# An encoder layer on one core: dummy products ahead of the first sums, and another order of loads and products for the second pair of row tiles

## The chip, the core and the metric

The kernel runs on one core of a Trainium2 chip. The metric is the device time in microseconds (us) of one execution, median over runs. Engines are named as in the profile: PE (TensorE, matrix products), ACT (ScalarE), DVE (VectorE), POOL (GpSimd), and SP, whose queue issues most DMA transfers.

## What is computed

One encoder layer on x of 1024 rows by 2048 columns, all in 32-bit floats. What matters here is its beginning:

```python
mod = jax.nn.silu(c) @ w_ada + b_ada
shift, scale, gate = jnp.split(mod, 3, axis=-1)
h = rmsnorm(x, pre_g) * (1.0 + scale[:, None]) + shift[:, None]
proj = h @ w_in
```

Then come windowed attention, pooling, a gated merge and a product with w_out; the change touches none of them.

## The kernel before, in words

Products keep single precision by splitting each operand into a high part, rounded to the format that PE takes at full speed (fp32r), and a low part, the rest; a product is high by high, high by low and low by high. Most of proj is made with Strassen's seven products of blocks (line 237). Ahead of that stands a ramp, in which data arrive while PE is already at work: for the first weight tiles of 256 columns (called tile i here, i = 0 to 3), plain blocks (line 833) are made from the first four row tiles of the weights, k = 0 to 3, taken as pair one (k = 0, 1; j = 0 in the code) and pair two (k = 2, 3; j = 1). The 1024 rows of x form two halves, s = 0 and 1, of 512. A block is named by weight half and x half: "11", "21" (x half 0), "12", "22" (x half 1); one block of one tile and one pair is six products of 512 columns.

Before the operands can be made, the scale is needed by columns of w_ada: `row_sums` multiplies silu(c) with w_ada on PE (tiles GEMV, line 539, four column groups), ACT copies the sums (acc, line 543), PE turns them (PM, line 523), DVE adds them up (pm, line 525) and makes `modc` (line 550). This is done for pair one and, by `scales[1]`, for pair two.

x is turned by PE (`turn_part`, tile XT, line 502, 128x128 transposes into a PSUM bank) and taken out by `take_turned` to the SBUF tiles xT (ACT line 510, DVE line 508). `raw_operands` multiplies by the scale column: the high part on ACT (B11h, B21h, B12h, B22h; line 695), the low part on DVE (B11l and so on; line 696). With `turned=True` it reads the PSUM bank, else the copy xT. `wide_weights` splits weights: high part whi on ACT (line 816) or DVE (814), low part wlo on DVE (line 106). `square_of` sums squares of x for the norm, on ACT (line 457) or DVE (454). `hold` copies a finished block from PSUM (line 837). The line `root` (931) makes ACT load its square-root table early.

`keep` pins an instruction: pinned instructions of an engine stand in the order of the calls. Each engine works through its own queue in order, and SP issues loads in the order of the calls, eight in flight. Loads are called in this order: 8 tiles of w_ada for the first scale, x columns 0 to 255 of rows 0 to 511 in four loads, half of the first weights, whole quarters (512 columns) of x of rows 512 to 1023, columns 256 to 511 of rows 0 to 511, the other half of the weights, 8 tiles for the second scale, the weights of pair two (`fetch_wide(0, 1)`), further x.

## Time and profile before

| | |
|---|---|
| time, median of 3 runs | 2085.4 us (2083.93 to 2087.7) |
| the profiled execution: time | 2086.17 us |
| its span, first to last instruction | 2084.4 us |
| PE busy | 2067.4 us, 99% |
| DVE, ACT busy | 1567.6 us (75%), 1110.7 us (53%) |
| mean granted clock of TensorE | 0.999 |

The span leaves out what lies around the instructions. Busy shares are of the span. The ramp's part that the change rewrites is the first 35 us or so.

### The profile page before, as it was taken

How to read it: one execution, taken by the hardware profiler on the slowest of the kernel's cores; microseconds unless marked ns; L12 is line 12 of the kernel's file. 1: busy time of each engine (PE TensorE's matmuls, PEld its weight loads, DVE VectorE, ACT ScalarE, POOL GpSimd, SP SyncE). 2: the span in 40 equal slices, each digit the busy share in tenths (PEclk: the TensorE clock that was granted, in tenths of full speed). 3: DMA queues.
4: the chain of work that ended last, by engine and by line, in shares of the span. 5: the costliest groups of instructions: out<-in, count | busy, mean ns of one | idle time of the engine just before them, and what ended most of it. 6: DMA issues, size and time to landing. Idle time of an engine off the chain costs nothing.

```text
span 2084.4 us, 29055 instructions
## 1 busy us (share of the span) xinstructions
PE 2067.4 (99%) x9527; PEld 1701.9 (82%) x9527; DVE 1567.6 (75%) x2823; ACT 1110.7 (53%) x2120; POOL 37.7 (2%) x132
## 2 busy tenths in 40 slices
PE   8999999999999999999999999999999999999998
PEld 6778888888888888888888888888888888888886
DVE  5889778776565876777777688857868977889667
ACT  5764444444664634655665444334645644768554
POOL 0100000000000000000000000010000000000000
PEclk9999999999999999999999999999999999999999
DMA  9978877887665477655554577665655556786897
GB/s 341 358 268 265 276 245 246 296 288 228 201 217 176 152 263 255 200 164 178 184 168 147 183 228 227 209 235 194 228 173 162 180 193 202 228 305 207 294 334 248
DMA packets 303137, 476.61 MB, mean 229 GB/s; under 512 B 24026, under 2 KB 140402, under 8 KB 302984
## 3 DMA queue, kind: packets, MB, share of 16 engines
q1 hardware_dynamic: 297616, 459.89, 67.3%
q0 software_dynamic: 4304, 12.75, 1.6%
q10 hardware_dynamic: 1064, 2.11, 0.3%
q8 instruction: 75, 1.23, 0.2%
q14 instruction: 78, 0.64, 0.1%
HBM read 346.70 MB, written 130.05 MB: 229 GB/s over the span
## 4 chain that ended last, share of the span: by engine, by line
PE 93%; DMA 3%; DVE 2%; ACT 1%; issue 0%; SPq 0%; DVEq 0%; ACTq 0%
PE Z L237 31%; PE V L237 20%; PE X L237 20%; PE Z L1704 2%; PE Z L1706 2%; PE Z L1705 2%; PE X L1706 1%; PE X L1704 1%; PE X L1705 1%; PE V L1704 1%; PE V L1705 1%; PE V L1706 1%; PE PB L833 1%; PE PT L1414 1%; DMA xt<-in_x_dram 1%; PE PV L1425 0%
## 5 line engine op out<-in xcount | busy, mean ns | idle before, releaser
L96 ACT ACTIVATE whi<-raw 128x512 fp32r<-128x512 f32 (+1 forms) x528 | 314.9, 600 | 488.6 <-PE Z L237 253.0
L97 DVE TENSOR_TENSOR wlo<-raw,whi 128x512 fp32r<-128x512 f32 (+1 forms) x528 | 339.9, 649 | 140.2 <-PE Z L237 109.9
L97 DVE TENSOR_TENSOR wlo<-wr,whi 128x512 fp32r<-128x512 f32 x224 | 150.5, 689 | 51.2 <-ACT whi L96 48.1
L96 ACT ACTIVATE whi<-wr 128x512 fp32r<-128x512 f32 x224 | 138.4, 629 | 87.3 <-DVE wlo L97 30.0
L103 DVE TENSOR_TENSOR raw<-raw,raw 128x512 f32<-128x512 f32 x76 | 52.4, 690 | 81.3 <-DMA raw<-in_w_merge_dram 51.6
L96 ACT ACTIVATE whi<-ws 128x512 fp32r<-128x512 f32 (+1 forms) x88 | 53.0, 602 | 72.9 <-PE X L237 61.4
L237 PE MATMUL Z<-T1h,whi 128*128 128x512 f32 x328 | 89.7, 390 | 0.3 <-ACT u L251 0.3
L237 PE MATMUL Z<-B22h,whi 128*128 128x512 f32 x328 | 89.6, 392 | 0.0
L237 PE MATMUL Z<-T2h,wlo 128*128 128x512 f32 x328 | 88.9, 390 | 0.6 <-DVE wlo L97 0.6
L237 PE MATMUL X<-B21h,whi 128*128 128x512 f32 x328 | 89.5, 391 | 0.0
L237 PE MATMUL V<-T4h,whi 128*128 128x512 f32 x328 | 89.5, 392 | 0.0
L237 PE MATMUL X<-B11h,whi 128*128 128x512 f32 x328 | 89.4, 390 | 0.0
L237 PE MATMUL Z<-T2h,whi 128*128 128x512 f32 x328 | 89.0, 390 | 0.4 <-ACT Z L293 0.3
L237 PE MATMUL V<-T3h,whi 128*128 128x512 f32 x328 | 89.3, 391 | 0.0
L237 PE MATMUL X<-B11l,whi 128*128 128x512 f32 x328 | 89.2, 390 | 0.0
L237 PE MATMUL Z<-B22l,whi 128*128 128x512 f32 x328 | 88.9, 390 | 0.0
L237 PE MATMUL Z<-T1l,whi 128*128 128x512 f32 x328 | 88.9, 389 | 0.0
L237 PE MATMUL X<-B21l,whi 128*128 128x512 f32 x328 | 88.9, 390 | 0.0
L237 PE MATMUL V<-T3l,whi 128*128 128x512 f32 x328 | 88.9, 390 | 0.0
L237 PE MATMUL V<-T4l,whi 128*128 128x512 f32 x328 | 88.9, 390 | 0.0
L237 PE MATMUL V<-T4h,wlo 128*128 128x512 f32 x328 | 88.8, 390 | 0.0
L237 PE MATMUL X<-B11h,wlo 128*128 128x512 f32 x328 | 88.8, 390 | 0.0
(421 smaller groups left out, 4910.3 us busy)
## 6 DMA issues: line engine op xcount, KB each, us to landing
part<-part_d SPq DMA_DIRECT2D x136, 256.0 KB, 4.7
ada<-in_w_ada_dram SPq DMA_DIRECT2D x128, 256.0 KB, 5.6
raw<-in_w_merge_dram SPq DMA_DIRECT2D x64, 512.0 KB, 5.2
wr<-ws_dS SPq DMA_DIRECT2D x60, 512.0 KB, 5.4
raw<-in_w_in_dram SPq DMA_DIRECT2D x56, 512.0 KB, 4.3
wr<-in_w_out_dram SPq DMA_DIRECT2D x48, 512.0 KB, 5.2
proj_d<-part SPq DMA_DIRECT2D x68, 256.0 KB, 2.4
sw<-in_w_out_dram SPq DMA_DIRECT2D x64, 256.0 KB, 5.2
```

The source lines that it names most:

```text
L96: ins = (nc.scalar.activation(hi, src, AF.Copy), nc.vector.tensor_tensor(lo, src, f32(hi), ALU.subtract))
L97: nc.vector.tensor_tensor(lo, src, f32(hi), ALU.subtract))
L103: return (eng or nc.vector).tensor_tensor(o, a, b, ALU.add)
L237: nc.tensor.matmul(ps, w_[:, i], op[mov][j][m_], start=fresh and i == 0 and n == 0, stop=i == nj - 1 and n == 2, skip_group_check=True)
L833: keep(nc.tensor.matmul(opened[i, blk], w[:, kh, nt * P:(nt + 1) * P], mov[kh][m], start=j == n == 0, stop=j == 1 and n == 5, skip_group_c ...
L1414: nc.tensor.transpose(pt[:, i * P:(i + 1) * P], p[:, i * P:(i + 1) * P], ident)
L1704: nc.tensor.matmul(pb, hi, w[0], start=first, stop=False, skip_group_check=True)
L1705: nc.tensor.matmul(pb, lo, w[0], start=False, stop=False, skip_group_check=True)
L1706: nc.tensor.matmul(pb, hi, w[1], start=False, stop=last, skip_group_check=True)
```

## The change

- `ones` is filled by DVE ahead of `scz`, not by POOL. `warm` (products of the tile `ones` with itself, 128x128, results unused) moves up and is called with 6 ahead of the turning of c, 3 behind it, and 1 after each of the first two steps of the first sums.
- The first sums are turned ahead of the x transposes, and `sum_columns` turns them into the free part of the sums' own PSUM bank.
- All x quarters 0 are loaded in halves of 256 columns. The second halves move behind the second scale: rows 0 to 511 ahead of the weights of pair two, rows 512 to 1023 behind them.
- The first weights are split by row tile (`first_weights`), and the products of pair one are reordered around the transposes of x half 1.
- Tile 1's blocks of pair one ("11", and "21" in two parts) stand ahead of and behind the second sums. Pair two's transposes move behind the second sums, its operands are read from the PSUM banks (`turned=True`), its weights are split by DVE, and its blocks "11", "21" of tile 0 stand among the transposes. The squares of x quarter 0 follow.

The core of the diff:

```diff
+    ones = xa2.tile([P, P], F32, name="ones")
+    nc.vector.memset(ones, 1.0)
     nc.vector.memset(scz, 0.0)
-    ones = xa2.tile([P, P], F32, name="ones")
-    nc.gpsimd.memset(ones, 1.0)
...
+    warm(6)
     pc = bank(SEEDED[1], "pc")
...
+    warm(3)
     scales = [fetch_scales(0)]
-    fetch_halves(0)
+    fetch_halves(range(4), 0)
     fetch_wide(0, 0, 0, 256)
-    for si in range(4, 8):
-        fetch_row(si, (0,))
-    fetch_halves(1)
+    fetch_halves(range(4, 8), 0)
     fetch_wide(0, 0, 256, 512)
...
     scales.append(fetch_scales(1))
+    fetch_halves(range(4), 1)
     fetch_wide(0, 1)
+    fetch_halves(range(4, 8), 1)
...
+    def first_weights(kh):
+        if kh == 0:
+            weights0[0, 0] = [wp.tile([P, 2, 256], F32R, tag=t, name=uid(t), bufs=4) for t in ("whi", "wlo")]
+        hi, lo = (t[:, kh] for t in weights0[0, 0])
+        keep(nc.vector.tensor_copy(hi, wide[0, 0][:, kh, 0:256]))
+        low_weights(lo, wide[0, 0][:, kh, 0:256], hi)
...
-    g[0]()
-    g[1]()
+    for q in range(2):
+        g[q]()
+        warm(1)
     g[2]()
     small_vectors()
     g[3]()
+    g[4]()
     turn_part(0, (0,), SEEDED[:1])
-    g[4]()
     turn_part(0, (1,), SEEDED[1:])
-    wide_weights(0, 0, True)()
-    raw_operands(0, 0, True)
+    for kh in range(2):
+        first_weights(kh)
+        raw_operands(0, 0, True, (kh,))
...
-    for n in (2, 1, 3):
+    for n in (2, 4):
         for blk, _ in PAIR:
             plain_block(0, blk, 0, None, (n,))
     turn_part(1, (0, 1), ("at", "at"))
-    for blk, _ in PAIR:
-        plain_block(0, blk, 0, None, range(4, 6))
+    for n in (1, 3, 5):
+        for blk, _ in PAIR:
+            plain_block(0, blk, 0, None, (n,))
...
-    turn_part(1, (2, 3), ("at", "at"))
-    turn_part(0, (2, 3), SEEDED)
-    for n in (1, 0):
-        for k in (2, 3):
-            take_turned(n, k, k == 3)
-    wide_weights(1, 0)()
-    for si in range(2):
-        square_of(si, 0, si % 2 == 1)
+    low()
+    plain_block(1, "11", 0, SEEDED[0])
+    plain_block(1, "21", 0, SEEDED[1], range(2))
     g = row_sums(scz, scales[1], partial(scale_columns, 1), 2)
     for step in g[:4]:
         step()
-    plain_block(1, "11", 0, SEEDED[0], range(2))
+    turn_part(0, (2,), ("at",))
     g[4]()
-    wide_weights(0, 1)()
-    raw_operands(1, 0)
-    raw_operands(1, 1)
+    wide_weights(0, 1, True)()
+    plain_block(1, "21", 0, None, range(2, 6))
+    turn_part(0, (3,), ("at",))
+    raw_operands(1, 0, True)
+    for k in (2, 3):
+        take_turned(0, k, False)
+    square_of(0, 0, False)
+    for n in (0, 2, 1, 3):
+        for blk, _ in PAIR:
+            plain_block(0, blk, 1, None, (n,))
+    turn_part(1, (2,), ("at",))
+    turn_part(1, (3,), ("at",))
+    raw_operands(1, 1, True)
+    for k in (2, 3):
+        take_turned(1, k, k == 3)
+    square_of(1, 0, True)
+    for n in (4, 5):
+        for blk, _ in PAIR:
+            plain_block(0, blk, 1, None, (n,))
     for si in range(2, 8):
         square_of(si, 0, si % 2 == 1)
     keep(nc.scalar.activation(ep.tile([P, 1], F32, name="root"), eps_t, AF.Sqrt))
-    plain_block(1, "11", 0, None, range(2, 6))
-    plain_block(1, "21", 0, SEEDED[1])
     wide_weights(1, 1)()
     norm_row(0)
-    plain_block(0, "11", 1)
     hold(0, "11")
-    plain_block(0, "21", 1)
     hold(0, "21")
```

How the engines' queues change, at the three places of which the prediction speaks. First PE's opening, before (pc is the turned c; GEMV the first sums, two products for each tile of w_ada, named ada):

```order
L776 MATMUL pc_140<-ident,crow 128x16
L539 MATMUL GEMV_377<-ada_144,scz 32x256 x2
L539 MATMUL GEMV_377<-ada_146,scz 32x256 x2
L539 MATMUL GEMV_377<-ada_148,scz 32x256 x2
L539 MATMUL GEMV_377<-ada_150,scz 32x256 x2
L539 MATMUL GEMV_377<-ada_152,scz 32x256 x2
```

and with the change (WARM takes the dummy products):

```order
L785 MATMUL WARM_140<-ones 128x128 x6
L789 MATMUL pc_147<-ident,crow 128x16
L785 MATMUL WARM_151<-ones 128x128 x3
L541 MATMUL GEMV_392<-ada_155,scz 32x256 x2
L541 MATMUL GEMV_392<-ada_157,scz 32x256 x2
L785 MATMUL WARM_397<-ones 128x128
L541 MATMUL GEMV_392<-ada_159,scz 32x256 x2
L541 MATMUL GEMV_392<-ada_161,scz 32x256 x2
L785 MATMUL WARM_403<-ones 128x128
```

Eleven dummy products stand ahead of and among the sums' products; nothing is taken out.

Second, ACT from pair two's operands to the high part of tile 1's weights, before (wide_245 holds pair two's weights, XT are PSUM banks, xT their copies, xt is x, the brackets name what an instruction waits for):

```order
L816 ACTIVATE whi_530<-wide_245 128x512 [waits DMAHW7_49]
L695 ACTIVATE B11h_213<-xT_191,modc 128x512 [waits DVE_49,Activation_49,Pool_49]
L695 ACTIVATE B21h_217<-xT_0_195,modc 128x512 [waits DVE_49,Pool_49]
L695 ACTIVATE B12h_225<-xT_193,modc 128x512 [waits Pool_49]
L695 ACTIVATE B22h_221<-xT_1_196,modc 128x512
L457 ACTIVATE xt_164,ssq_x<-xt_164 128x512 [waits DMAHW4_49,DMAHW3_49]
L457 ACTIVATE xt_170,ssq_x<-xt_170 128x512
L457 ACTIVATE xt_174,ssq_x<-xt_174 128x512 [waits DMAHW0_49]
L931 ACT_TABLE_LOAD
L931 ACTIVATE root<-eps_t 128x1
L816 ACTIVATE whi_561<-wide_245 128x512
```

and with the change, behind B11h and B21h of pair two:

```order
L510 ACTIVATE xT_198<-XT_524 128x512 [waits DVE_49]
L510 ACTIVATE xT_0_202<-XT_543 128x512 [waits DVE_49]
L457 ACTIVATE xt_171,ssq_x<-xt_171 128x512 [waits DMAHW3_49,DMAHW1_49]
L701 ACTIVATE B12h_232<-XT_563,modc 128x512 [waits PE_49,Pool_49]
L701 ACTIVATE B22h_228<-XT_568,modc 128x512 [waits PE_49]
L510 ACTIVATE xT_200<-XT_563 128x512 [waits DVE_49]
L457 ACTIVATE xt_175,ssq_x<-xt_175 128x512 [waits DMAHW5_49]
L457 ACTIVATE xt_181,ssq_x<-xt_181 128x512 [waits DMAHW6_49,DMAHW0_49]
L457 ACTIVATE xt_185,ssq_x<-xt_185 128x512 [waits DMAHW2_49]
L960 ACT_TABLE_LOAD
L960 ACTIVATE root<-eps_t 128x1
L837 ACTIVATE whi_592<-wide_256 128x512 [waits DMAHW7_49]
```

The split of the weights (first row before) has left ACT, and three copies xT<-XT that stood ahead of the second sums, with one square, stand between the operands or behind them.

Third, DVE from the second scale's sums on, before (pm are the sums, modc the scale):

```order
L525 TENSOR_REDUCE pm_526<-PM_523 128x2 [waits PE_49]
L550 TENSOR_SCALAR modc<-pm_526,b_128,cols 128x1 [waits DVE_49]
L550 TENSOR_SCALAR modc<-pm_526,b_128,cols 128x1
L106 TENSOR_TENSOR wlo_531<-wide_245,whi_530 128x512 [waits DMAHW7_49,Activation_49]
L696 SCALAR_TENSOR_TENSOR B11l_214<-xT_191,modc,B11h_213 128x512 [waits Activation_49,Pool_49]
L696 SCALAR_TENSOR_TENSOR B21l_218<-xT_0_195,modc,B21h_217 128x512 [waits Activation_49,Pool_49]
L696 SCALAR_TENSOR_TENSOR B12l_226<-xT_193,modc,B12h_225 128x512 [waits Activation_49,Pool_49]
L696 SCALAR_TENSOR_TENSOR B22l_222<-xT_1_196,modc,B22h_221 128x512 [waits Activation_49]
```

and with the change:

```order
L526 TENSOR_REDUCE pm_531<-GEMV_505 128x2 [waits PE_49,Activation_49]
L555 TENSOR_SCALAR modc<-pm_531,b_128,cols 128x1 [waits DVE_49]
L555 TENSOR_SCALAR modc<-pm_531,b_128,cols 128x1
L835 CAST whi_535<-wide_256 128x512 [waits DMAHW7_49]
L106 TENSOR_TENSOR wlo_536<-wide_256,whi_535 128x512 [waits DVE_49]
L702 SCALAR_TENSOR_TENSOR B11l_221<-XT_524,modc,B11h_220 128x512 [waits Activation_49,Pool_49]
L702 SCALAR_TENSOR_TENSOR B21l_225<-XT_543,modc,B21h_224 128x512 [waits Activation_49,Pool_49]
L702 SCALAR_TENSOR_TENSOR B12l_233<-XT_563,modc,B12h_232 128x512 [waits Activation_49,Pool_49]
L702 SCALAR_TENSOR_TENSOR B22l_229<-XT_568,modc,B22h_228 128x512 [waits Activation_49]
L508 COPY xT_1_203<-XT_568 128x512
```

The high part of the weights is made here (CAST), and the low operands are read from the banks XT instead of the copies xT.

## Rows read from the trace of the kernel before

**Rows 1.** The page: the chain that ended last, by engine.
```profile
PE 93%; DMA 3%; DVE 2%; ACT 1%; issue 0%; SPq 0%; DVEq 0%; ACTq 0%
```

**Rows 2.** Timeline of PE, 0 to 60 us: start, length, instruction, count, idle time before.
```profile
10.18 1.29 PE L539 MATMUL GEMV<-ada,scz 128*32 128x256 f32 x8
...
13.79 0.73 PE L833 MATMUL PB<-B11h,whi 128*128 128x512 f32 x2 [0.93 <-ACT B11h L695]
...
18.10 0.50 PE L833 MATMUL PB<-B22h,whi 128*128 128x512 f32 x1
...
20.71 1.91 PE L502 MATMUL XT<-ident,xt 128*128 128x128 f32 x16
22.55 2.04 PE L539 MATMUL GEMV<-ada,scz 128*32 128x256 f32 x32
...
28.14 0.49 PE L833 MATMUL PB<-B11h,whi 128*128 128x512 f32 x1 [0.33 <-ACT B11h L695]
...
34.11 0.39 PE L833 MATMUL PB<-B11h,whi 128*128 128x512 f32 x1
...
34.59 0.50 PE L833 MATMUL PB<-B11h,wlo 128*128 128x512 f32 x1
```

**Rows 3.** Line 539 (GEMV), 0 to 10 and 20 to 26 us: duration in ns, min/median/max.
```profile
L539 PE MATMUL GEMV<-ada,scz x24: 631/634/637, 3.7 to 9.3; 128*32 128x256 f32 x24
...
L539 PE MATMUL GEMV<-ada,scz x32: 379/379/403, 22.6 to 24.2; 128*32 128x256 f32 x32
```

**Rows 4.** Timeline of ACT, 0 to 60 us.
```profile
14.87 0.60 ACT L510 ACTIVATE xT<-XT 128x512 f32<-128x512 f32 x1 [0.56 <-DVE B11l L696]
...
22.55 0.60 ACT L510 ACTIVATE xT<-XT 128x512 f32<-128x512 f32 x1 [0.28 <-PE XT L502]
23.04 0.62 ACT L816 ACTIVATE whi<-wide 128x512 fp32r<-128x512 f32 x1
...
24.64 0.38 ACT L543 ACTIVATE acc<-GEMV 128x256 f32<-128x256 f32 x1 [0.37 <-PE GEMV L539]
26.85 0.63 ACT L816 ACTIVATE whi<-wide 128x512 fp32r<-128x512 f32 x1 [1.82 <-DMA wide<-in_w_in_dram]
...
29.84 0.62 ACT L457 ACTIVATE xt<-xt 128x512 f32<-128x512 f32 x1
...
33.19 0.62 ACT L816 ACTIVATE whi<-wide 128x512 fp32r<-128x512 f32 x1
```

**Rows 5.** Timeline of DVE, 0 to 60 us.
```profile
13.03 0.42 DVE L814 CAST whi<-wide 128x512 fp32r<-128x512 f32 x1
13.48 0.69 DVE L106 TENSOR_TENSOR wlo<-wide,whi 128x512 fp32r<-128x512 f32 x1
14.09 0.75 DVE L696 SCALAR_TENSOR_TENSOR B11l<-XT,modc,B11h 128x512 fp32r<-128x512 f32 x1
...
25.76 0.46 DVE L550 TENSOR_SCALAR modc<-pm,b,cols 128x1 f32<-128x1 f32 x2
...
33.84 0.69 DVE L106 TENSOR_TENSOR wlo<-wide,whi 128x512 fp32r<-128x512 f32 x1 [1.06 <-ACT whi L816]
```

**Rows 6.** Loads of the second scale, and of pair two's weights: issue, then time to landing.
```profile
L562 SPq DMA_DIRECT2D ada<-in_w_ada_dram x8: 368/467/467, 14.4 to 18.3; - x8
...
DMA to landing us min/median/max: 4.3/5.0/5.7
...
L772 SPq DMA_DIRECT2D wide<-in_w_in_dram x1: 467/467/467, 18.8 to 18.8; - x1
...
DMA to landing us min/median/max: 8.1/8.1/8.1
```

**Rows 7.** Windows: busy time of each engine, granted clock, DMA share, GB/s.
```profile
24.00:27.00 3.00, 3.00 (x24) 2.03 (x17) 1.62 (x6) 0.81 (x4) 0.00 (x0) 1.00 1.05 380
...
2080.00:2084.40 4.40, 0.00 (x0) 0.00 (x0) 0.54 (x1) 0.00 (x0) 0.00 (x0) 0.50 0.54 191
```

**Rows 8.** Timeline of PE, its last product.
```profile
2075.86 0.39 PE L1706 MATMUL Z<-wlo,mh 128*128 128x512 f32 x1
```

More of the change, by code (lines that the diff above doesn't have):

```diff
@@ L431, in fetch_row, with fetch_halves @@
             keep(load(xts[si, q], x[si * P:(si + 1) * P, q * 512:(q + 1) * 512]))
-    def fetch_halves(h):
-        for si in range(4):
+    def fetch_halves(sis, h):
+        for si in sis:
             if h == 0:
@@ L518, in ada_tile, with sum_columns @@
         return at
-    def sum_columns(acc, n=4):
-        pt = bank("at", "PM")
+    def sum_columns(acc, n=4, pt=None):
+        if pt is None:
+            pt = bank("at", "PM")
         for g in range(n):
@@ L524, in sum_columns @@
         pm = xa2.tile([P, 4], F32, tag="pm", name=uid("pm"), bufs=2)
-        keep(nc.vector.tensor_reduce(pm[:, 0:n], pt.rearrange("p (g k r) -> p g k r", g=4, k=4)[:, 0:n, :, 0],
+        keep(nc.vector.tensor_reduce(pm[:, 0:n],
+                                     pt[:, 0:n * P].rearrange("p (g k r) -> p g k r", g=n, k=4)[:, :, :, 0],
                                      op=ALU.add, axis=AX.X))
@@ L543, in step, with columns @@
                 keep(nc.scalar.activation(st_["acc"][:, 0:n], pv.rearrange("p (g n) -> p g n", g=n), AF.Copy))
-        return [partial(step, q) for q in range(kcs // 4)] + [lambda: then(sum_columns(st_["acc"], n))]
+        def columns():
+            then(sum_columns(st_["acc"], n, st_["pv"][:, n * P:2 * n * P] if n == 2 else None))
+        return [partial(step, q) for q in range(kcs // 4)] + [columns]
     def scale_columns(j, pm):
@@ L687, in encoder_layer, with raw_operands @@
     right = {}
-    def raw_operands(j, s, turned=False):
-        for kh, name in enumerate(("B11", "B21") if s == 0 else ("B12", "B22")):
+    def raw_operands(j, s, turned=False, khs=(0, 1)):
+        for kh in khs:
+            name = (("B11", "B21") if s == 0 else ("B12", "B22"))[kh]
             k = 2 * j + kh
@@ L773, in fetch_wide, with warm @@
                   w_in[2 * j * P:(2 * j + 2) * P, n0 + n1:n0 + n2].rearrange("(k p) n -> p k n", p=P)))
+    def warm(n):
+        b = bank("at", "WARM")
+        for _ in range(n):
+            keep(nc.tensor.matmul(b[:, 0:P], ones, ones, start=True, stop=True))
+    warm(6)
     pc = bank(SEEDED[1], "pc")
@@ L848, in put_by @@
         nc.gpsimd.dma_start(block(ramp_d[i], 0)(blk), t)
-    def warm(n):
-        b = bank("at", "WARM")
-        for _ in range(n):
-            keep(nc.tensor.matmul(b[:, 0:P], ident, ident, start=True, stop=True))
     BLOCKS = ("11", "21", "12", "22")
@@ L907, in encoder_layer @@
         take_turned(1, k, k == 1)
-    PAIR = (("12", "mm"), ("22", "mm"))
-    for blk, tag in PAIR:
+    low = wide_weights(1, 0)
+    for blk, tag in (("12", "mm"), ("22", "mm")):
         plain_block(0, blk, 0, tag, range(2))
-    for blk, _ in PAIR:
+    for blk in ("12", "22"):
         plain_block(0, blk, 0, None, range(2, 6))
-    turn_part(1, (2, 3), ("at", "at"))
-    turn_part(0, (2, 3), SEEDED)
-    for n in (1, 0):
-        for k in (2, 3):
-            take_turned(n, k, k == 3)
-    wide_weights(1, 0)()
-    for si in range(2):
-        square_of(si, 0, si % 2 == 1)
+    low()
+    plain_block(1, "11", 0, SEEDED[0])
+    plain_block(1, "21", 0, SEEDED[1], range(2))
     g = row_sums(scz, scales[1], partial(scale_columns, 1), 2)
```

## The prediction, made before the change was run

> **What bounds the kernel now.** I read the page first, then the timelines of PE, ACT and DVE over the first 40 us, then the DMA issues there. The page shows PE busy 99% of the span (the table above) and 93% of the chain that ended last [rows 1]: whatever the ramp (the stage up to about 77 us that the change rewrites) does to the moment at which PE ends its ramp work is handed on to the end, and nothing else of the ramp counts. So the question is at which places of the ramp PE is held, by whom, and where it is held afterwards.
>
> In PE's timeline [rows 2] the reader is to see four things. The last eight products of the first scale's sums (GEMV, from 10.18) take 1.29 us, and 32 of them at 22.55 take 2.04. The first product of pair one comes at 13.79, after 0.93 us of idle time, released by ACT's B11h. At 18.10 PE has again been held for a third of a microsecond by ACT (B22h). At 28.14 it is held by ACT's B11h of pair two. Then it runs without a hole to 34.59, where the third product of tile 1's first block of pair two (the first two from 34.11) begins, the first one that takes the low part of those weights: that low part left DVE at 33.84 + 0.69 = 34.53 [rows 5], so PE and the two helpers arrive there together. This is the place that decides my forecast.
>
> **The first us.** GEMV products last 0.63 us in the first ten us and 0.38 later [rows 3]. The page's slices give the granted clock as full from the start, so I go by the durations: the early ones run at the lower level, 1.2 GHz, the later ones at 2.4. Eleven dummy products of 128x128, six of them ahead of everything, on a tile that DVE fills first, keep PE at work from about 1 us on. I take it that the clock is then up when the last two scale tiles land. Their landing is not moved (the first 13 loads keep their places), so the eight products that take 1.29 us can shrink to 2.04/4 = 0.51 at best, and by nothing at worst; I take 0.5 us, since they cannot start ahead of their data. The sums' two transposes no longer stand behind four of x: 0.1 us. First product of pair one at 13.2 instead of 13.79. The dummies' own time lies in waits for the scale's tiles and costs nothing, unless the clock stays low; then the two single ones cost at most two fp32 products of half a GEMV's width, some 0.8 us, ahead of tiles that arrive every 0.75 us, and the 13.2 is 13.8 again.
>
> **Pair one.** The first weights are split by halves and the low products of B11 stand ahead of the transposes of the other half of x, so the hold at 18.10 (0.3 us) goes. PE ends the four blocks of tile 0 at about 19.85 instead of 20.71. Then eight products of tile 1 (8 x 0.24 = 1.9 us, by 34.11 to 34.59 for two) take the place of 16 transposes (1.91 us, from 20.71), since those move behind the scale's sums. Second GEMV at 21.75 instead of 22.55; its data, 1 MB earlier in SP's queue than before, are there. Up to here the change gains 0.8 us. ACT's copy of the sums, their transposes and DVE's modc follow as before (24.64 to 25.76 [rows 4, 5]) and end at 25.4.
>
> **Pair two's operands.** Before, B11h of pair two waited for the weights (wide, issued at 18.77, 8.1 us to landing [rows 6]), and ACT began at 26.85. Now half of x (0.5 MB) stands behind the weights instead of ahead; at 380 GB/s that is 1.4 us [rows 7], so they land at about 25.4. DVE makes high and low part (0.45 and 0.61 from start to start at 13.03 and 13.48 [rows 5]) and B11l from 26.45 to 27.2, B21l from 27.1 to 27.85. ACT begins B11h at 25.35 and B21h at 25.95, two us ahead of before.
>
> But what follows on ACT is longer. The operands are now taken out of the PSUM banks of the transposes, and the copies of those banks to xT, which stood ahead of the second sums (one at 22.55 [rows 4], where ACT waited for PE), now stand between B21h and B12h, with a square, and one more behind B22h. The row at 14.87 [rows 4] shows such a copy held 0.56 us until DVE's B11l, which reads the same bank, had ended (14.09 + 0.75 [rows 5]). So the first copy starts at 27.2, the second at 27.85, the square 0.49 later (a copy at 22.55, the next work at 23.04 [rows 4]), B12h at 28.95, B22h at 29.55; the third copy waits for B12l (29.65 + 0.75 = 30.4) and ends its turn at 30.9. Three squares, the table load and root take 3.35 us (29.84 to 33.19): the high part of tile 1's weights starts at 34.25, where it started at 33.19 [rows 4]. PE, by then done with the blocks of tile 0 at some 32.9 (34.11 before), stands still for 2 us. The low part follows 0.65 after the high one and lasts 0.69, and the product that stood at 34.59 begins at 35.65.
>
> The Trainium skill, PSUM — Partial Sum Buffer, section PSUM bank collisions raise a hardware error, asks for order between any two engines on one bank, a read of ACT against a read of DVE included; it speaks against reading operands and copies out of the same banks. By it the three copies wait as worked out, and the sum is +1.05; without it ACT would run through and the sum would be -0.1. The row at 14.87 agrees with it.
>
> **The sum.** Gains of 0.6, 0.3 and 0.1 us on PE are all ahead of 33 us and end in the 2 us that PE stands still; what is left is ACT's lag, 35.65 - 34.59 = +1.05 us. From there PE has no reserve to give back (it is 99% busy), and ACT's later work in the ramp moves by the same 1.05. The execution of the profile took 2086.17 us (span 2084.4 and 1.8 around it): 2087.2 with the change. That execution is 0.8 over the median of the three runs, 2085.4, so I forecast **2086.4 us**. The lower bound of the term is ACT without any wait: 25.35, operands 1.2, two copies 1.0, square 0.6, operands 1.2, copy 0.5, and 3.35 for squares, table and root make 33.2, no difference (-0.1 with the shorter PSUM reads). The upper bound is the weights landing as late as before, 18.8 + 8.1 = 26.9: everything behind DVE's split moves by 1.4, and the term is +2.45. I take 1.05, by the landing worked out and the held copy. Four more loads on SP (halves for whole rows) cost nothing: SP stood waiting for landings between its issues, and eight loads stay in flight. Ones filled by DVE instead of GpSimd: nothing, both idle there.
>
> **Rivals.** A: ACT keeps pace. If the copies are not held, or the sums come half a microsecond earlier, the high part of the weights is ready at 32.7 to 33.2 and PE's lead survives in part: between 0 and -1.2 us (PE's own arrival, 32.9 against 34.11); I put it at -0.6, 2084.8. For it: PE's lead is solid. Against: the copy at 14.87.
>
> B: the data come late. The load of the weights took 8.1 us before; if it and the second half of x behind it land at 26.9 or later, the transposes, B12h and all behind them wait, +2.45 us, 2087.9. For it: the weights landed 2.9 us behind the last tile of the scale, the load ahead of them (18.8 + 8.1 against 18.3 + 5.7), which at 380 GB/s is the time of 1.1 MB for 0.5 MB [rows 6]. It decides from a landing at 25.4 on, microsecond for microsecond.
>
> C, the other side: the stall of 2 us lets the clock fall. Then PE works at 1.2 GHz from about 35 us, as it did up to 11.5. If it lasts as long as from the first GEMV to the end of the last one, 3.7 to 11.47 [rows 2, 3], half of 7.8 us is lost: +3.9, 2090.3, slower by 0.24%. It needs a stall clearly longer than my 2 us: the one fall in this trace, to 0.50 in 2080 to 2084.4, comes behind the end of all PE work at 2076.25 [rows 7, 8], and after the hold at 13.79 the clock was up [rows 2]. The Trainium skill, TensorE: Matmul & The Clock Gate, section HAM oscillation, warns of just such gaps between bursts; by it this stall is near the danger, and no row here has one of this length.
>
> D: the dummies do nothing. If the clock rises as late as before, the first term is 0 and everything behind the second GEMV is half a microsecond later: +1.55, 2086.9. The GEMV rows would show 0.63 to the end.
>
> **How the numbers follow.** Forecast 0.48, A 0.21, B 0.14, C 0.08, D 0.09. What a measurement of this kernel can tell from no change is about 0.2%, 4.2 us: below 2081.2 or above 2089.6. The forecast, A, B and D lie within; C lies above. Single runs shown lie between 2083.93 and 2087.7, 1.5 below and 2.3 above the median; with that spread I give 0.04 to faster and 0.09 to slower, 0.87 to the middle. The range reaches from A less the lower spread, 2083.5, to B plus 0.9, 2088.8; left out are C and the tails, together under 0.2.
>
> **What would show it.** Right: GEMV rows of 0.38 us before 11 us; first product of pair one near 13.2; second GEMV near 21.75; a hold of PE near 33 us of some 2 us, released by ACT's whi of tile 1 at 34.25; ACT's copies of the transposed banks held by DVE's B11l and B21l. Wrong: no hold of PE at 33 us (A), the weights for pair two later than 26 us (B), products of 512 columns further apart than 0.24 us after 35 us (C), or GEMV rows of 0.63 at 10 us (D). If the hold at 33 us is there and the time is still 2 us or more shorter, a later stage gives time back that I take for lost.

## The result, and the profile after

The change made the kernel slower by some 3.4 us. In the first comparison its median was 2088.47 us (16 runs, 2084.99 to 2095.44) against 2085.03 for the kernel before (16 runs). The comparison puts the ratio of the times at 1.0020, 95% interval 1.0013 to 1.0028 (that of the two medians alone is 1.0016). Measured twice more among the experiments it stood at 1.0019 (1.0009 to 1.0028) and 1.0016 (1.0007 to 1.0025). The profiled execution took 2088.44 us (span 2086.7), where that of the kernel before took 2086.17 (span 2084.4). I had forecast 2086.4 and no difference that can be told; the measured time lies in my range, above the forecast.

PE's timeline of the changed kernel in the first us (start, length, instruction, count, idle time before it), to be read against [rows 2] (a product of two f32 tiles shows as two rows, so the first six dummies are x12):

```profile
1.09 2.93 PE L785 MATMUL WARM<-ones 128*128 128x128 f32 x12 [1.09 <-DVE ones L389]
...
7.93 0.63 PE L541 MATMUL GEMV<-ada,scz 128*32 128x256 f32 x4 [0.55 <-DMA ada<-in_w_ada_dram]
...
10.18 1.32 PE L541 MATMUL GEMV<-ada,scz 128*32 128x256 f32 x8
...
13.86 0.50 PE L854 MATMUL PB<-B11h,whi 128*128 128x512 f32 x1 [0.57 <-DVE wlo L106]
```

And the durations of the first sums' products (ns, min/median/max; first and last start), to be read against [rows 3]:

```profile
L541 PE MATMUL GEMV<-ada,scz x30: 379/403/436, 5.7 to 10.9; 128*32 128x256 f32 x30
```

The products of the sums now last 0.38 to 0.44 us from the first one on, where they lasted 0.63: the clock is up. (The rise in the table below is the first entry of the trace's record of the granted clock. Ahead of it the windows view prints 1.00, though in the kernel before the products last 0.63 there.) But the last eight start at 10.18 and take 1.32 us as before, since the last tile of the scale landed at 10.82 in this execution (10.37 before), and pair one begins at 13.86, not earlier than before.

ACT's timeline, to be read against [rows 4]:

```profile
25.87 0.69 ACT L701 ACTIVATE B11h<-XT,modc 128x512 fp32r<-128x512 f32 x1 [1.19 <-DVE modc L555]
...
27.69 1.26 ACT L510 ACTIVATE xT<-XT 128x512 f32<-128x512 f32 x2 [0.37 <-DVE B11l L702]
...
31.03 0.60 ACT L510 ACTIVATE xT<-XT 128x512 f32<-128x512 f32 x1 [0.31 <-DVE B12l L702]
...
33.48 1.28 ACT L960 ACT_TABLE_LOAD   x1
34.77 0.20 ACT L960 ACTIVATE root<-eps_t 128x1 f32<-128x1 f32 x1
34.88 0.61 ACT L837 ACTIVATE whi<-wide 128x512 fp32r<-128x512 f32 x1
```

The copies out of the transposes' banks are held until DVE has made its low parts (B11l, B12l) out of the same banks, and the high part of tile 1's weights starts at 34.88 (33.19 in [rows 4], 34.25 in my forecast). What PE does meanwhile, against [rows 2]:

```profile
22.27 1.93 PE L541 MATMUL GEMV<-ada,scz 128*32 128x256 f32 x32
...
33.19 0.40 PE L854 MATMUL PB<-B22l,whi 128*128 128x512 f32 x1
35.55 0.50 PE L854 MATMUL PB<-B11h,whi 128*128 128x512 f32 x1 [1.96 <-ACT whi L837]
35.89 0.40 PE L854 MATMUL PB<-B21h,whi 128*128 128x512 f32 x1
36.28 0.57 PE L854 MATMUL PB<-B11h,wlo 128*128 128x512 f32 x1
36.64 0.63 PE L854 MATMUL PB<-B21h,wlo 128*128 128x512 f32 x1
37.07 0.63 PE L854 MATMUL PB<-B11l,whi 128*128 128x512 f32 x1
...
39.63 0.56 PE L854 MATMUL PB<-B11l,whi 128*128 128x512 f32 x1
40.02 0.40 PE L854 MATMUL PB<-B21l,whi 128*128 128x512 f32 x1
```

PE stands for 1.96 us ahead of tile 1's first block of pair two. Its third product, the place on which my sum was made, starts at 36.28 (34.59 before: +1.69). Then the products, which have been 0.23 us apart, are 0.43 apart. The windows view shows why (columns: stretch, its length, busy time of PE, PEld, DVE, ACT, POOL, granted clock, DMA share, GB/s):

```profile
33.42:35.55 2.13, 0.17 (x2) 0.00 (x1) 1.29 (x7) 2.10 (x5) 0.00 (x0) 1.00 1.02 375
35.55:36.57 1.02, 1.02 (x3) 0.59 (x4) 1.02 (x2) 1.02 (x4) 0.00 (x0) 1.00 1.05 406
36.57:39.98 3.41, 3.41 (x9) 2.67 (x9) 2.08 (x7) 3.38 (x11) 0.00 (x0) 0.50 1.06 394
39.98:42.00 2.02, 2.02 (x10) 1.62 (x9) 1.99 (x6) 1.99 (x6) 0.00 (x0) 1.00 1.05 386
```

One us behind the stand the granted clock falls to 0.50 (1.2 GHz) for 3.41 us, in which eight products start instead of some fifteen, and is then back at 1.00 (2.4 GHz). As the mark for the end of the ramp I take the first product of T2, one of Strassen's sums of blocks (line 237): 77.35 before, 80.21 now, +2.86. PE's timelines, first the kernel before, then the change:

```profile
77.35 0.73 PE L237 MATMUL Z<-T2h,whi 128*128 128x512 f32 x2 [0.25 <-ACT Z L293]
```

```profile
80.21 0.73 PE L237 MATMUL Z<-T2h,whi 128*128 128x512 f32 x2 [0.19 <-ACT Z L293]
```

The rest of the program, from that product to PE's last end, takes as long in the one as in the other, to 0.5 us:

```profile
77.35:2076.25 1998.90, 1996.21 (x9149) 1652.16 (x9149) 1513.89 (x2705) 1059.16 (x2011) 28.40 (x67) 1.00 0.68 224
```

```profile
80.21:2078.59 1998.38, 1995.71 (x9149) 1651.78 (x9149) 1511.78 (x2705) 1059.53 (x2011) 28.45 (x67) 1.00 0.68 224
```

So this pair of profiles puts the loss into the ramp: 1.69 us up to 36.28, where ACT's queue holds PE (0.45 of it is the later landing of the scale in this execution), and 1.17 us more behind it, at the lower clock.

### The profile page after: what moved, and what is told of

Its sections match the earlier page's. It is cut to its first block, busy times and chain, and to the rows that moved or that the text cites. A ratio compares the mean times of both kernels' runs of the same rounds, so it can differ in the third digit from the quotient of the medians.

```text
span 2086.7 us, 29102 instructions
## 1 busy us (share of the span) xinstructions
PE 2070.9 (99%) x9549; PEld 1706.7 (82%) x9549; DVE 1565.4 (75%) x2826; ACT 1111.2 (53%) x2120; POOL 37.7 (2%) x131
## 3 DMA queue, kind: packets, MB, share of 16 engines
q8 instruction: 75, 1.23, 0.2%
## 4 chain that ended last, share of the span: by engine, by line
PE 94%; DMA 2%; DVE 2%; ACT 1%; issue 0%; SPq 0%; DVEq 0%; ACTq 0%
PE Z L237 31%; PE V L237 20%; PE X L237 20%; PE Z L1729 2%; PE Z L1731 2%; PE Z L1730 2%; PE PB L854 2%; PE V L1729 1%; PE X L1729 1%; PE X L1730 1%; PE V L1730 1%; PE X L1731 1%; PE V L1731 1%; DMA raw<-in_w_merge_dram 1%; PE PT L1439 1%; PE PV L1450 0%
## 5 line engine op out<-in xcount | busy, mean ns | idle before, releaser
L237 PE MATMUL Z<-T1h,wlo 128*128 128x512 f32 x328 | 88.8, 389 | 0.0
```

The lines of the kernel that those rows point to most:

```text
L237: nc.tensor.matmul(ps, w_[:, i], op[mov][j][m_], start=fresh and i == 0 and n == 0, stop=i == nj - 1 and n == 2, skip_group_check=True)
```

## Experiments

Theory S: ACT's queue makes PE stand, and the stand lets the clock fall. Against it stood, one after the other, D (the dummies' early rise of the clock, not the stand, brings the fall), L (the loads, more and smaller, set the ramp) and V (the dummies cost time behind the ramp). A stand is a stretch in which PE waits. The table has, for one profiled execution of each kernel: landing of the first scale's last tile, rise of the clock, first product of pair one, longest stand of PE between 27 and 53 us and its end, stretch at half rate in the ramp, first T2 product; and the ratio of the times to those of the kernel before in the same call, with its interval (10 to 16 runs each).

| kernel | tile | rise | first | stand, end | half rate | T2 | ratio |
|---|---|---|---|---|---|---|---|
| before | 10.37 | 11.32 | 13.79 | 0.33, 28.14 | none | 77.35 | 1 |
| e17 before itself | 10.69 | 10.30 | 14.06 | 0.08, 36.35 | none | 76.74 | 1.0000 (0.9991 to 1.0009) |
| the change | 10.82 | 5.85 | 13.86 | 1.96, 35.55 | 36.57 to 39.98 | 80.21 | 1.0020 (1.0013 to 1.0028) |
| e5 change again | 10.32 | 5.86 | 13.36 | 1.95, 35.05 | 36.58 to 39.99 | 79.71 | 1.0019 (1.0009 to 1.0028) |
| e18 change, third | 9.98 | 5.32 | 13.02 | 1.97, 34.71 | 36.04 to 39.45 | 79.36 | 1.0016 (1.0007 to 1.0025) |
| e1 weights first | 10.18 | 4.84 | 13.22 | 2.64, 38.33 | 38.98 to 42.39 | 80.00 | 1.0013 (1.0004 to 1.0022) |
| e2 stand filled | 9.95 | 10.52 | 13.56 | 0.14, 38.67 | none | 78.73 | 1.0025 (1.0016 to 1.0034) |
| e3 no dummies | 9.85 | 7.34 | 12.88 | 1.98, 34.56 | 34.65 to 38.06 | 78.95 | 1.0005 (0.9996 to 1.0014) |
| e12 no dummies | 10.21 | 9.92 | 13.25 | 1.94, 34.96 | none | 79.92 | 1.0017 (1.0008 to 1.0026) |
| e16 thin dummies | 10.38 | 16.45 | 14.35 | 1.96, 36.99 | none | 80.48 | 1.0026 (1.0017 to 1.0035) |
| e4 ACT's order | 10.12 | 5.31 | 13.16 | 2.12, 44.55 | 46.27 to 49.68 | 79.82 | 1.0031 (1.0022 to 1.0041) |
| e6 order, mended | 10.47 | 6.25 | 13.50 | 1.19, 50.74 | none | 78.65 | 1.0022 (1.0013 to 1.0030) |
| e7 e6, no dummies | 10.65 | 16.30 | 14.62 | 1.24, 52.62 | none | 80.20 | 1.0010 (1.0001 to 1.0020) |
| e9 e6, whole rows | 9.88 | 14.12 | 14.49 | 1.23, 51.74 | none | 79.33 | 1.0012 (1.0003 to 1.0021) |
| e10 e9, no dummies | 9.96 | 9.19 | 13.00 | 1.25, 51.24 | none | 78.81 | 1.0009 (0.9999 to 1.0018) |
| e11 whole rows | 10.58 | 5.60 | 13.62 | 1.96, 36.89 | none | 80.38 | 1.0016 (1.0007 to 1.0026) |
| e8 before + dummies | 10.38 | 5.00 | 13.79 | 0.05, 36.97 | none | 77.03 | 1.0004 (0.9995 to 1.0014) |
| e13 the same again | 10.58 | 5.82 | 13.96 | 0.05, 36.64 | none | 76.68 | 1.0010 (1.0002 to 1.0019) |
| e14 before, ones by DVE | 10.55 | 12.61 | 14.31 | 0.04, 36.55 | none | 76.62 | 1.0005 (0.9997 to 1.0014) |
| e15 before + thin dummies | 10.09 | 13.03 | 14.05 | 0.05, 36.87 | none | 77.01 | 1.0012 (1.0001 to 1.0022) |

**e1, the weights first.** Against the change:

```diff
+    wide_weights(1, 1)()
     for si in range(2, 8):
         square_of(si, 0, si % 2 == 1)
     keep(nc.scalar.activation(ep.tile([P, 1], F32, name="root"), eps_t, AF.Sqrt))
-    wide_weights(1, 1)()
```

> The high part of tile 1's weights (pair two) stands ahead of the six squares and the table load on ACT. Theory S (ACT's queue makes PE stand, and the stand lets the clock fall) comes in two forms. S-place: only the place of these weights counts; PE then has no hold at 33.4, the clock stays up, the first T2 product of the ramp is near 77.3 (80.21 in the change) and the time is near 2085.5. S-queue: all of ACT's work up to the copy that frees the next bank (held, 38.35 in the change) counts; the hold only moves, to some 36.2, and lasts some 2.7 us until 38.95; the T2 product stands at 79.0 without a fall of the clock, 80 to 80.5 with one, and the time is 2087 to 2088.5. I expect S-queue. Rival D (the fall is owed to the dummy products' early rise of the clock, not to the stand): half-rate products from 36.57 on again, wherever the hold is.

PE's timeline of e1:

```profile
35.30 0.39 PE L854 MATMUL PB<-B21l,whi 128*128 128x512 f32 x1
38.33 0.50 PE L854 MATMUL PB<-B12h,whi 128*128 128x512 f32 x1 [2.64 <-ACT held L858]
38.67 0.40 PE L854 MATMUL PB<-B22h,whi 128*128 128x512 f32 x1
38.90 0.55 PE L854 MATMUL PB<-B12h,wlo 128*128 128x512 f32 x1
39.25 0.63 PE L854 MATMUL PB<-B22h,wlo 128*128 128x512 f32 x1
```

S-queue: the weights come early enough, and PE stands 2.64 us at the next thing that ACT owes it, the bank that `hold` empties. The half-rate stretch came with the stand, 2.4 us later than in the change, so D, which wanted it at 36.57, falls here. The time, 2089.42, lies above the 2087 to 2088.5 that I expected.

**e2, the stand filled.** `warm(9)` ahead of `plain_block(1, "11", 1)`.

> Nine more dummy products of 128x128 stand on PE just ahead of tile 1's first block of pair two, where PE stands for 2.1 us in the change: nothing that ACT does moves. Theory S: PE is at work through the wait, no product behind it goes at half rate (0.43 us apart), the lag that ACT set stays (third product near 36.3, T2 product near 79.0, so 1.2 less than the 80.21 of the change), time about 2087.2. Rival D: the half-rate stretch from 36.57 to 39.98 is there all the same, T2 product at 80.2 or later, time as the change or a little more.

PE's timeline of e2:

```profile
33.10 2.17 PE L785 MATMUL WARM<-ones 128*128 128x128 f32 x18
35.24 0.50 PE L854 MATMUL PB<-B11h,whi 128*128 128x512 f32 x1
35.58 0.40 PE L854 MATMUL PB<-B21h,whi 128*128 128x512 f32 x1
35.97 0.50 PE L854 MATMUL PB<-B11h,wlo 128*128 128x512 f32 x1
36.31 0.39 PE L854 MATMUL PB<-B21h,wlo 128*128 128x512 f32 x1
```

Nothing but PE's idleness was taken away, the wait for ACT stays, and there is no half-rate stretch. From the first product of pair one to the T2 product it is 65.17 us, in the three traces of the change 66.34 to 66.36: 1.18 us less, as expected. One trace does not show that the filling did it, since e11, e12 and e16 below have the same stand unfilled and no fall either. It takes all twenty traces: a fall in the ramp stands behind six of the nine stands of 1.9 us or more, and in none of the eleven traces without such a stand.

The price of the fall is shown by e11 and e16, which have the same stand and the same products behind it, but no fall. PE's timeline of e11:

```profile
36.89 0.50 PE L854 MATMUL PB<-B11h,whi 128*128 128x512 f32 x1 [1.96 <-ACT whi L837]
...
39.78 0.39 PE L854 MATMUL PB<-B21l,whi 128*128 128x512 f32 x1
40.32 0.50 PE L854 MATMUL PB<-B12h,whi 128*128 128x512 f32 x1
```

The block's twelfth product starts 2.89 us behind the stand's end here, 4.47 in the change (40.02 less 35.55): 1.58 lost. At the next block e11, e16 and e2 all wait for 0.14 or 0.15 us while PE in the change comes later and does not, and 0.41 of the loss is given back. The T2 product comes 43.49 us behind the first product of tile 1's block in e11, e16 and e2, 44.65 to 44.67 in the three traces of the change: the fall costs 1.17 (0.90 in e3, at 44.39, where it begins 0.09 us behind the stand).

The times did not follow: 1.0025, where some 1.0008 was due, and no better than the change. The profiled execution (2087.72) was the shortest of the eleven. What the others lose, and where, no trace shows.

**e3 and e12, no dummies.** All four `warm` calls left out.

> The change without any of its eleven dummy products. Theory S: the first scale's sums run at the lower level (0.63 us a product), their end moves by 0.0 to 0.3 us since they wait for their data, the stand at 33.4 is there again with 1.7 to 2.2 us, and half-rate products follow it: T2 product at 80.0 to 80.6, time 2088 to 2089. Rival D: without the early rise the clock does not fall after the stand: T2 product near 79.0, time 2087.2, so the dummies cost 1.2 us.

> The change without its dummy products once more, for the spread (1.0005 of the kernel before at first, where the change itself stood at 1.0020 and 1.0019). Theory S: a stand of 2 us and a fall of the clock as with dummies, T2 product at 79 to 81 by the rise of the clock, ratio 1.001 to 1.002. Rival V: 1.0005 again.

The stand is there in both, so the dummies don't make it. In e3 the clock fell behind it without them: D falls for good. In e12, the same kernel, it did not fall. The T2 product of e3 (78.95) missed its bound by a us, because its scale landed at 9.85 and its clock rose by itself at 7.34. In e12 something else ended the ramp, in ACT's timeline:

```profile
68.27 0.42 ACT L96 ACTIVATE whi<-raw 128x256 fp32r<-128x256 f32 x1 [1.63 <-DMA raw<-in_w_in_dram]
```

The first weights of the next stage landed at 68.25 (65.03 before, 66.25 in the change), and the T2 product came out as late as with a fall. That is what L says, in one execution; but in e3 the same loads landed at 66.50, so chance alone can do it.

**e4, ACT's order turned round.** The copies of finished blocks ahead of squares and table load:

```diff
-    for si in range(2, 8):
-        square_of(si, 0, si % 2 == 1)
-    keep(nc.scalar.activation(ep.tile([P, 1], F32, name="root"), eps_t, AF.Sqrt))
     wide_weights(1, 1)()
-    norm_row(0)
     hold(0, "11")
     hold(0, "21")
-    norm_row(1)
+    for si in range(2, 4):
+        square_of(si, 0, si % 2 == 1)
     plain_block(0, "12", 1)
     hold(0, "12")
...
+    wide_weights(2, 0)()
+    keep(nc.scalar.activation(ep.tile([P, 1], F32, name="root"), eps_t, AF.Sqrt))
+    norm_row(0)
```

> ACT's (and DVE's) order after the operands of pair two is turned round: tile 1's high part first, then the copies of tile 0's blocks as each ends, with squares and the table load between and behind them. Same work on every engine. Theory S (both forms): no hold at 33.4, no hold at 36 to 39, clock up throughout, third product of tile 1's first block near 33.9 to 34.2 (36.28 in the change, 34.59 before), T2 product at 76.5 to 77.2 unless the squares, now later, hold the factors of the norm (needed near 52); time 2084.3 to 2085.3, 3 to 4 less than the change and at or 1 below the kernel before. Rival D: a half-rate stretch in the 30s even so, T2 product 1.2 later. Rival L (late loads, not ACT, set the ramp): T2 product stays within 0.5 of 79.

PE's timeline of e4:

```profile
44.55 0.50 PE L854 MATMUL PB<-B11h,whi 128*128 128x512 f32 x1 [2.12 <-ACT whi L837]
...
46.76 0.63 PE L854 MATMUL PB<-B21h,whi 128*128 128x512 f32 x1
```

No stand up to 42 us, and then the same stand at tile 2's second weights, which I had left behind four rows' squares; the clock fell behind it again. ACT had itself stood for 1.68 us until the load of tile 2's first weights landed (36.91), so that this stand is not its queue's alone. The expectation was wrong; the fall behind a stand was the same.

**e5, e18: the change again.** No edit.

> The change itself, unaltered, on the chip of the next three, for its spread and a second trace. Theory S: PE stands again for 1.7 to 2.2 us ahead of tile 1's first block of pair two, 3.4 us at half rate follow it, first T2 product of the ramp at 79.3 to 80.3 by the landing of the scale's last tile (10.82 in the first trace; 0.9 earlier in others). Time 1.001 to 1.002 of the kernel before. If there is no fall of the clock behind a stand of that length, theory S loses its second half.

> The change, unaltered, for the third time. By theory S its mean stands 2 to 3 us over e17 (the ramp's lag in two traces was 2.4 and 2.9 us); by V 3.5 to 4. A stand of 2.1 us ahead of tile 1's first block is there; half-rate products behind it in most executions.

The stand and the half-rate stretch are in both: in three of three traces of the change. In the means of their runs the three measurements stand 3.90, 3.87 and 3.10 us over the kernel before (standard error 0.8 to 1.0 each). Over e17 alone, as the expectation of e18 has it, it is 3.71: nearer to V's 3.5 to 4 than to the 2 to 3 of S, with an error of 1.0 that does not tell them apart.

**e6, e7: the order mended, with dummies and without.** As e4, with `root` and `norm_row(0)` ahead of `wide_weights(2, 0)`, and `wide_weights(2, 1)` ahead of rows 2 and 3.

> ACT's order turned round again, with the table load ahead of the load that the last try stood waiting for, and both weights of tile 2 ahead of the rows' squares. Theory S: no stand of over 0.5 us between 27 and 48 us, no half-rate stretch, first T2 product at 76 to 77 (77.35 before, 80.21 in the change); a stand of up to 1 us at the factors of the norm (RB, near 50) is possible since the squares end later. Time 0.999 to 1.0005 of the kernel before if the ramp is all that counts. Rival V (the runs with dummies lose time at a place that the traces so far don't show): 1.001 or more all the same.

> The same order of ACT without any dummy products. Theory S: as with them, first T2 product at 76 to 77.3, time 0.999 to 1.0005. Rival V: this one 2 us or more faster than the same order with dummies; by S alone the two differ by under 0.7 us either way (the rise of the clock against their own time).

PE's timeline of e6:

```profile
49.17 0.39 PE L854 MATMUL PB<-B22l,whi 128*128 128x512 f32 x1
50.74 1.98 PE L490 MATMUL RB<-diag,ones 128*128 128x512 f32 x4 [1.19 <-ACT diag L483]
```

No stand before 49 us, no fall of the clock, as expected; e7, whose first product came at 14.62 with the late rise of the clock, shows the same. But the squares, now behind, make the norm's factors late, and PE stands for them. T2 came at 78.65, not at 76 to 77. Whichever work of ACT and DVE I put first, the wait turned up at what I put last.

**e9, e10, e11: whole rows of x.**

```diff
-    fetch_halves(range(4, 8), 0)
+    for si in range(4, 8):
+        fetch_row(si, (0,))
...
-    fetch_halves(range(4, 8), 1)
```

> The order of e6 (with the dummy products), but x of the lower four row tiles is loaded in whole rows of 512 columns again, as before: four loads fewer. Theory L (beside S: smaller loads cost SP and the transfers time, so that everything loaded behind them is later; the last rows of x landed at 45.6 to 47.1 in the change and its variants, 44.8 in the kernel before): the second scale lands up to 1.3 us later, the second sums' products start near 23 instead of 22, but the last x row lands at 44.7 to 45.5, the stand at the factors of the norm (RB, 1.35 in e6) shrinks to under 0.7, and the first T2 product is at 77.0 to 77.8 (78.65 in e6). Rival (the later landings are slow stretches of the transfers that come by chance): last row of x at 45.6 to 47.1 as without, T2 product at 78.5 to 79.5. Time 1.0003 to 1.0015 of the kernel before by L, 1.001 to 1.002 by the rival.

> The same without dummy products. Theory L: last x row at 44.7 to 45.5, T2 product at 77 to 78.3 (the clock's rise, left to itself, came at 7.3, 11.3 and 16.3 us so far), time 0.9998 to 1.001. Rival V (runs with dummies are slower somewhere behind the ramp): 2 us less than e9 although its ramp is no shorter.

> The change with whole rows for the lower four row tiles and nothing else. Theory S: ACT's operands of pair two start up to 1.3 us later (the scale lands later), the stand ahead of tile 1's first block is 2 to 3 us, half-rate products follow, T2 product at 80 to 81.5, time 1.0015 to 1.003: the halves by themselves were worth it in this order. Theory L: last x row at 44.7 to 45.5 all the same.

The last recorded row of x landed at 43.64 in e9 and 43.97 in e10 (47.11 in e6, 45.60 in e7, 44.77 before), earlier than L asked, yet the stand at the factors stayed at 1.23 and 1.25, so that stand is ACT's and DVE's and not the loads'. In e11, with the stand at 36.89, the same loads were as late as in the change (46.86). In these traces the rows come early only with both, whole rows and no stand; with one of the two alone (e11; e6, e7) they land at 45.6 to 47.1. One or two traces of each do not show that this is more than chance. The T2 products of e9 and e10 (79.33, 78.81) came later than L asked.

**e8, e13 to e15, e17: the kernel before, with dummies, with its ones filled by DVE, and unaltered.** e8 and e13 add the four `warm` calls and the fill by DVE; e15 cuts each dummy to 16 columns; e14 has the fill alone; e16 is the change with dummies of 16 columns.

> The kernel before with the change's eleven dummy products, the ones written by DVE, and nothing else of the change. My forecast's first term: the clock is up before the first scale's last products, first product of pair one 13.3 to 13.5 (13.79 before), time 0.3 to 0.5 us less, within what can be measured. Rival V: the dummies alone cost 1 to 2.5 us (ratio 1.0005 to 1.0012). Theory S says nothing here: no stand over 1.1 us in this order.

> The kernel before with the eleven dummy products once more (first time: mean 1.7 us over before, ratio 1.0004). Rival V: 1 to 2.5 us over the kernel before, with the ramp no longer than its 77.35 (first T2 product 76.8 to 77.4): the cost is behind the ramp, in stands of PE near 260 or 434, 511 and 848 us. Rival N (the excess was chance): within 0.7 us of before.

> The kernel before with the ones written by DVE ahead of the zeros instead of by GpSimd, no dummy product. Control: no difference, within 0.7 us, by every theory; if it costs 1 us or more, the fill and not the products was what e8 measured.

> The kernel before with the eleven dummies cut to 16 columns each: the same instructions, an eighth of the work. V by work: no cost, within 0.7 us, and the clock rises as late as without (11 us). V by presence: 1 to 2.5 us as with the full ones. N: within 0.7 us.

> The change with its dummies cut to 16 columns. Theory S: the stand of 2 us ahead of tile 1's first block is there, with or without half-rate products behind it (7 stands of 2.1 to 2.8 us in the ramp so far, 5 followed by them), T2 product at 79 to 80.3. Time by S alone 1.6 to 2.9 us over before; by V through work the same, 1.5 less than the change; by V through presence 3.4 to 4 as the change.

> The kernel before, unaltered. Theory F (the footing: one more kernel comes out longer than the many runs of before): 1 to 2 us over the runs of before, ratio 1.0005 to 1.001; then nothing is left that the dummies cost. Rival V (the fill or the dummies' presence costs): within 0.5 us of the runs of before, ratio 0.9996 to 1.0003.

In the old order the dummies raise the clock at 5.0 and 5.8 and gain nothing: the first product stays at 13.79 in e8. The sums are copied out at 11.10 there (11.52 before), but the turning of them stands behind x's transposes and begins at 12.04 in both. In the means, e8, e13 and e15 stand 1.67, 2.04 and 2.49 us over the runs of before, the control e14 1.17, before itself 0.61 under (each with a standard error of 0.5 to 0.9), while none of their ramps is longer. By the bound set for e14, 1 us, the fill by DVE and not the products would be what e8 measured; 1.17 with an error of 0.5 does not settle that, and over e14 the three stand only 0.5 to 1.3 us. Thin dummies cost no less than full ones, so it is hardly their work (e16, too, stands 5.21 over before, above every figure expected of it), and by e17 a kernel does not come out longer merely because it is one more. V is neither shown nor ruled out. What makes these kernels 1 to 2.5 us longer behind the ramp, and e2, e4 and e6 some 3, stays open. e16 shows the stand once more without a fall. PE's timeline of e16, and its window from the stand's end on, at a granted clock of 1.00:

```profile
36.99 0.50 PE L854 MATMUL PB<-B11h,whi 128*128 128x512 f32 x1 [1.96 <-ACT whi L837]
37.33 0.40 PE L854 MATMUL PB<-B21h,whi 128*128 128x512 f32 x1
37.72 0.50 PE L854 MATMUL PB<-B11h,wlo 128*128 128x512 f32 x1
38.05 0.39 PE L854 MATMUL PB<-B21h,wlo 128*128 128x512 f32 x1
```

```profile
36.99:41.00 4.01, 3.87 (x15) 2.59 (x16) 2.67 (x8) 3.98 (x11) 0.00 (x0) 1.00 1.05 387
```

No version beat the kernel before.

## Why the prediction was right or wrong

**The first us: the mechanism right, the landing not mine to count on.** The clock rose at 5.3 to 5.9 us in the change's traces, as supposed. From the landing of the scale's last tile to the first product it takes 3.04 us in all three, 3.42 before: 0.4 gained. It is the clock's: from the landing to ACT's copy of the sums it takes 0.72 us, where it took 1.15 in the first trace of before. By e8 the clock alone does not bring it through; the sums have to be turned ahead of x. My 0.6 supposed the landing of the one trace, 10.37; it was 10.82, 10.32 and 9.98, and the first product came at 13.86, 13.36 and 13.02. In the execution that was profiled first, the term was zero.

**Pair one: right.** The second sums start 8.41 us behind the first product (8.76 before, 8.55 in my working).

**ACT's lag: right, and nearly to the digit.** From the second sums to the third product of tile 1's first block I had 13.9 us (35.65 less 21.75); it was 14.01 (36.28 less 22.27), and 12.04 before (10.99 in e17, where pair two's weights landed at 25.54 and not 26.82, so that the base of this term hung on one landing too). The held copies, the stand of 2 us and its releaser are in the trace as described. Here my reading of the Trainium skill, PSUM — Partial Sum Buffer, section PSUM bank collisions raise a hardware error, held: the copies stand at 27.69 and 31.03 behind DVE's reads of the same banks.

**The clock: the step that failed.** In the sum the clock behind the stand of 2 us stood at nothing; it took 1.17 us. I wrote of rival C that it "needs a stall clearly longer than my 2 us", gave it 0.08 and priced it at 3.9 us. It came in all three traces of the change, behind a stand of 2 us, and in e1, e3 and e4 (stands of 2.64, 1.98 and 2.12). I had only one fall to go by, the one at the end of all work, and one hold of 0.93 us without a fall [rows 2, 7, 8]; between 0.93 and 2 us I had no row, and took the far one. The price was too high: the fall lasted 3.41 us, not 7.8. In it 1.58 us were lost, and 0.41 of these PE would have spent behind ACT at the next block anyway: against e2, e11 and e16, and by the traces (2.86 less 1.69), the fall cost 1.2. The Trainium skill, TensorE: Matmul & The Clock Gate, section HAM oscillation, which I cited and set aside, warns of gaps between bursts. The waits of its example, some 3 to 5 us, are longer than the 2 us here, so that it did not foretell this fall. And three stands of 1.94 to 1.96 us (e11, e12, e16) were followed by none: which stand has one behind it is not worked out here.

**No reserve behind the ramp: right.** What was lost by the T2 product was still lost at PE's last end (+2.86, +2.34).

**The loads: open.** "Four more loads on SP cost nothing" holds for the change itself, whose ramp was ended by other things. The first weights of the next stage landed late in two variants (66.98 in e6, 68.25 in e12, 65.03 before), and ACT waited for them in both; but in e7, with the same loads, they landed at 65.57 and ACT did not wait. That the smaller loads do it is not shown.

**The sum.** My +1.05, with the clock's 1.17 and the 0.64 that was missing up to 36.28 (the first product 0.66 later than my 13.2, pair one 0.14 shorter, ACT's lag 0.11 longer), makes the +2.86 of the trace. The traces of the change put T2 at 79.76 in the mean, the two of the unaltered kernel before at 77.05: 2.7 us. The times say 3.1 to 3.9, with an error of 0.8 to 1.0; what is left, 0.4 to 1.2 us, is hardly clear of that error and is not explained. Two smaller slips: the range's lower end by its own terms is 2083.3 (2084.8 less 1.5), and what can be told from no change, put at 4.2 us, was far less, since the interval came out at 1.0013 to 1.0028.

## What to carry to other kernels

Read a stand of PE as two costs, its length and what the clock may take behind it (0.9 to 1.2 us where it could be measured; a fall came behind six of nine stands of 1.9 to 2.6 us). If the wait can't be removed, filling it with work is worth a try, but it is not shown to pay: e2's one trace had no fall, and its times came out no better. Before work is moved ahead on the engine that bounds, add up the whole queue of the helper that feeds it, copies held by another engine's reads and table loads with it: where that helper has no slack, as ACT, which was busy for 2.10 of the 2.13 us around the stand, a new order chooses where the wait appears (33, 36, 42 or 49 us here). And take more than one trace before a term is hung on a single landing: the same tile landed between 9.85 and 10.82 us.

## What the runs showed of the hardware

The rise and the fall of the clock move from run to run. With full dummies from 1.09 us on, the clock rose at 4.8 to 6.3 us in nine traces and at 10.5 and 14.1 in two (e2, e9); without, or with thin ones, anywhere from 7.3 to 16.5. The ten falls ahead of the program's end (six between 34 and 50 us, four near 848, in e8, e9, e12 and e14) all lasted 3.41 us and began 0.1 to 2.1 us behind a stand of 1.4 us or more. Stands of that length without a fall there are too, up to 2.35 us (at 850 us in e6). The Trainium skill, TensorE: Matmul & The Clock Gate, section What's actually happening, says that the point of the change varies from run to run of one kernel, by some half a microsecond either way; these traces agree that it varies, but with full dummies two of eleven lie 4 to 8 us later than the rest.

Most of the spread in these traces was not the clock. In the longer executions PE stands at a few places far behind the ramp. From the T2 product to PE's last end e9 takes 8.3 us longer than e10, and 5.2 of them are three stands. PE's timeline of e9 (span 2092.4):

```profile
262.48 0.72 PE L237 MATMUL V<-T3h,whi 128*128 128x512 f32 x2 [1.12 <-DVE u L103]
...
513.26 0.39 PE L1226 MATMUL GATE<-sel,folds 128*16 128x32 f32 x8 [2.29 <-DVE folds L1220]
...
849.93 0.39 PE L1420 MATMUL SCORE<-k,qhi 128*128 128x256 f32 x1 [1.78 <-ACT k L96]
```

The last of these waits for ACT, which waits 1.02 us for a load. In e10 (span 2083.6), the same kernel without dummies, the first and the third are not there at all and the second lasts 0.17 us; e6, e8 and e12 have stands of 1.81 to 2.48 us at the third place. They move between executions of one kernel as well: the first profile of before has 0.75 us at the third place and 0.17 at the second, e17 has 0.34 and 1.53. A ramp that ends 1 us sooner can so be hidden in one pair of executions by later stands, and a kernel of this length wants its stages compared apart.
